# A hybrid attention block: the heads' stacked query and key operands by way of DRAM, and the causal mask inside the scan

## The chip, the cores and the metric

The kernel runs on one core of a Trainium2 chip. TensorE (PE) multiplies, VectorE (DVE), ScalarE (ACT) and GpSimd (POOL) do the elementwise work, SyncE (SP) issues most of the DMAs, and POOL issues some. The metric is the device time of one execution in microseconds (us); lower is better. A profile is one more execution, in which every instruction is recorded.

## The reference, cut to what matters

One layer of a decoder with 1024 tokens and a width of 1024. A norm and one wide projection give queries, keys and values for two kinds of attention, and two gates. The dilated attention has 12 heads in three groups; the stick-breaking attention has 8 heads. Both outputs are projected up, gated, added, projected again, and an MLP with a hidden width of 4096 follows.

```python
z = jnp.einsum('bhqd,bhkd->bhqk', q_blk, kt).astype(jnp.float32) * scale
causal = key_pos[None, :] < q_pos[:, None]
log_one_minus = jnp.where(causal, jax.nn.log_sigmoid(-z), 0.0)
suffix = lax.cumsum(log_one_minus, axis=3, reverse=True) - log_one_minus
log_a = jax.nn.log_sigmoid(z) + suffix
a = jnp.where(causal, jnp.exp(log_a), 0.0)
```

In the dilated heads the scores `q.k/8` get a bias that falls with the distance and go through a softmax over a window; groups 1 and 2 take every 4th or every 16th token, so their tokens are put into another order first.

## The kernel before, in words

Every float32 matmul is made of three products of halves: a value is rounded to a high part (an ACT copy, names with `h`), and the rest is the low part (a DVE subtraction, names with `l`).

**Two heads at a time.** A head is 64 wide and a tile has 128 partitions, so the projection of q (or k) for a pair of heads comes out as a [128, 1024] matrix with one head in partitions 0 to 63 and the other in 64 to 127. It comes in two column halves of 512 tokens. A score matmul of one head contracts over 128 partitions, and what lies in them is stacked: `qs` holds the high part of q on the head's own 64 partitions and the low part on the other 64, `kk` holds the high part of k on both, and `kl` holds the low part of k on the head's own 64 partitions and zeros on the others. `scores` (L850) then needs two matmuls, `qs` by `kk` and `qs` by `kl`.

**Who builds them.** In `qk_pair` (L800) the inner `sink` gets a column half of q or k. For every head it copies 64 partitions with ACT (k twice, once on each half), and subtracts 64 partitions with DVE. In groups 1 and 2 (pairs D2 to D5) each of these is two instructions, since the token order is changed by strided reads (`perm_dst`, L776). POOL clears the zero half of `kl` (L811). There are six dilated pairs, D0 to D5, and four stick-breaking pairs, S0 to S3. For the stick-breaking pairs the plain projection goes to DRAM first (`sb_pair`, `zdr`, L786 to 793), and `sb_load` (L795) reads it back when the heads are about to run; the `sink` works at that time.

**Stick breaking.** `sb_front` (L984) does, for each block of 128 queries: scores into PSUM, a sigmoid by ACT into `be`, on the block's last 128 columns a mask by POOL (`affine_select` writes 1 where the key is not before the query, L998), and a DVE scan from right to left (`tensor_tensor_scan`, multiply by `be` and add a zero, L1004). `sb_back` transposes the result, splits it and multiplies it by the values.

**What sets the order.** Nothing is issued as it is written. Class `Plan` (L65) records every operation, gives it a cost (`cost`, L186), a due time that follows from PE's order, and a window; `issue` (L222) then runs a list schedule in which each engine takes the ready operation that is due first, and emits a fixed order for each engine. A DMA is taken in the plan as 360 bytes per ns after 650 ns. All engines, SP's queue included, then run their own fixed order and wait on semaphores. `FILL` (L56) is the queue of projections that are slipped between the attention heads (`d1`, `s2` and so on); `ORDER` (L55) is the order of the heads. All working tiles share one pool of 102 slots.

Of the kernel before, what the change touches and what calls it, by code (L numbers as in the profile page):

```python
# [15 lines left out]
S = 1024  # L16
# [48 lines left out]
class Plan:  # L65
# [120 lines left out]
    def cost(eng, method, out, args, kw):  # L186
# [35 lines left out]
    def issue(self):  # L222
# [42 lines left out]
        ready = {}  # L265
# [116 lines left out]
def hybrid_block(ctx, tc, xT, w_t, w_vn, w_up, w_o, w_mi, w_mo, gains, bgate, out):  # L382
# [403 lines left out]
    zdr = dram.tile([4, 2, 2, 128, 512], F32, name="zdr")  # L786

    def sb_pair(n):
        def sink(i, c, src):
            if "PSUM" in str(src.tensor.space):  # L790
                src = keep(src)
            sync.dma_start(zdr[n, i, c], src)
        return seven((18 + n, 22 + n), sink)

    def sb_load(n, i, c):  # L795
        t = u2("sq", F32)
        sync.dma_start(t, zdr[n, i, c])
        return t

    def qk_pair(tq, tk, g, res, strassen, load=None):  # L800

        qs = [[u2("qs") for _ in range(2)] for _ in range(2)]
        kk = [[u2("kk") for _ in range(2)] for _ in range(2)]
        kl = [[u2("kl") for _ in range(2)] for _ in range(2)]
        res.extend((qs, kk, kl))

        for hd in range(2):
            for t in kl[hd]:  # L810
                pool.memset(f(t[64 * (1 - hd):64 * (1 - hd) + 64]), 0.0)  # L811

        def sink(i, c, ps):
            src = nat_src(ps, g)
            todo = []
            for hd in range(2):
                a, b = 64 * hd, 64 * (1 - hd)
                kld = perm_dst(kl[hd], g, c)
                for (dst, sl), (dl, _) in zip(perm_dst((kk if i else qs)[hd], g, c), kld):
                    sv = src[a:a + 64, sl] if g else src[a:a + 64]  # L820
                    if i:
                        act.activation(dst[a:a + 64], sv, AF.Copy)
                        act.activation(dst[b:b + 64], sv, AF.Copy)
                        todo.append((dl[a:a + 64], sv, f(dst[a:a + 64])))
                    else:
                        act.activation(dst[a:a + 64], sv, AF.Copy, scale=-0.125)
                        todo.append((dst[b:b + 64], sv, f(dst[a:a + 64])))
            for dst, sv, hi in todo:
                e = eng(SLE if load else DSE if "PSUM" not in str(ps.tensor.space) else "d")
# [5 lines left out]
        if load:  # L835
            for i in range(2):
                for c in range(2):
                    sink(i, c, load(i, c))
                    yield
            return  # L840
# [9 lines left out]
    def scores(ps, qk, hd, q0, k0, n):  # L850

        qs, kk, kl = qk
        qt, qo = qs[hd][q0 // 512], q0 % 512
        ki, ko = k0 // 512, k0 % 512
        pe.matmul(ps, qt[:, qo:qo + 128], kk[hd][ki][:, ko:ko + n], start=True, stop=False)
        pe.matmul(ps, qt[:, qo:qo + 128], kl[hd][ki][:, ko:ko + n], start=False, stop=True)
# [17 lines left out]
    def dil_head(g, slot, qk, vs, ut, dense):  # L874
# [5 lines left out]
        for c in range(2):  # L880
            es = {}
            for bk in range(2 if g < 2 else 1):
# [4 lines left out]
                if g < 2:  # L887
                    for j in range(2):
# [7 lines left out]
                        if k0 // 512 != (k0 + w - 1) // 512:  # L896
                            scores(sc[:, o0:o0 + 128], qk, hd, 128 * b, k0, 128)
# [652 lines left out]
```

## Time and profile before

| | us |
|---|---|
| median of 3 runs | 1509.33 |
| lowest and highest | 1506.43, 1511.13 |
| the profiled execution | 1508.43 |
| its span, first to last instruction | 1506.7 |

The page of the profile gives, for each engine, the time in which it was busy and the number of its instructions, then the granted TensorE clock, the DMA queues, the waits and the costliest groups of instructions. A view by stretches cuts the span and gives the same for each piece; a view of groups by form gives the mean time of one instruction of each shape. "DMA share" is the mean busy share of the core's 16 DMA engines, so that one engine alone is 0.06. Line 378 stands for all instructions, since the plan emits them there; so groups are told apart by the names of their tiles.

### The profile page before, as it was taken

How to read it: one execution, taken by the hardware profiler on the slowest of the kernel's cores; microseconds unless marked ns; L12 is line 12 of the kernel's file. 1: busy time of each engine (PE TensorE's matmuls, PEld its weight loads, DVE VectorE, ACT ScalarE, POOL GpSimd, SP SyncE). 2: the span in 40 equal slices, each digit the busy share in tenths (PEclk: the TensorE clock that was granted, in tenths of full speed). 3: DMA queues.
4: the chain of work that ended last, by engine and by line, in shares of the span. 5: the costliest groups of instructions: out<-in, count | busy, mean ns of one | idle time of the engine just before them, and what ended most of it. 6: DMA issues, size and time to landing. Idle time of an engine off the chain costs nothing.

```text
span 1506.7 us, 22489 instructions
## 1 busy us (share of the span) xinstructions
PE 1449.4 (96%) x7660; PEld 1231.9 (82%) x7660; DVE 1166.8 (77%) x2003; ACT 853.1 (57%) x1758; POOL 279.8 (19%) x322
## 2 busy tenths in 40 slices
PE   9999999899999999978999999999999999999997
PEld 8989887777787788756779978788888888888887
DVE  8798676987744498899999798666665969696876
ACT  8557667978544567764654464555555726262512
POOL 3674241222323333411140200000000000000000
PEclk9999999999999999999999999999999999999999
DMA  6403140131335644323513154444445917171603
GB/s 223 128 15 126 36 147 29 64 105 50 119 112 171 208 139 127 115 88 112 182 43 126 45 187 154 171 150 149 149 145 183 374 57 251 56 252 37 230 1 112
DMA packets 114900, 194.69 MB, mean 129 GB/s; under 512 B 14085, under 2 KB 29793, under 8 KB 114785
## 3 DMA queue, kind: packets, MB, share of 16 engines
q1 hardware_dynamic: 111456, 182.76, 36.0%
q0 software_dynamic: 3328, 10.49, 2.2%
q8 instruction: 60, 0.98, 0.3%
q14 instruction: 56, 0.45, 0.1%
HBM read 134.86 MB, written 58.34 MB: 128 GB/s over the span
## 4 chain that ended last, share of the span: by engine, by line
PE 68%; DVE 15%; ACT 7%; DMA 4%; issue 4%; POOL 1%; SPq 1%; DVEq 0%; POOLq 0%; ACTq 0%
PE bank L378 57%; PE vps L378 6%; DVE be L378 3%; ACT kk L378 3%; DVE ws L378 2%; DVE el L378 2%; PE po L378 2%; PE tr L378 1%; ACT e L378 1%; DMA vdr<-vt 1%; DVE tc L378 1%; DMA ws<-in_w_mi_dram 1%; PE sc L378 1%; DVE gl L378 1%; DVE hl L378 1%
## 5 line engine op out<-in xcount | busy, mean ns | idle before, releaser
L378 PE MATMUL bank<-hh,ws 128*128 128x512 f32 x1792 | 568.3, 394 | 5.3 <-ACT pk L378 2.7
L378 PEld LDWEIGHTS bank<-hh,ws 128*128 128x128 f32 x1792 | 336.4, 189 | 77.4 <-ACT pk L378 4.3
L378 DVE TENSOR_TENSOR ws<-ws 128x512 fp32r<-128x512 f32 (+3 forms) x520 | 344.8, 707 | 45.4 <-ACT ws L378 20.5
L378 PE MATMUL bank<-hl,ws 128*128 128x512 f32 x896 | 352.2, 393 | 0.0
L378 ACT ACTIVATE ws<-ws 128x512 fp32r<-128x512 f32 (+1 forms) x376 | 214.4, 607 | 161.9 <-PE bank L378 101.7
L378 PE MATMUL bank<-hi,ws 128*128 128x512 f32 (+1 forms) x976 | 285.1, 375 | 0.0
L378 PEld LDWEIGHTS bank<-hi,ws 128*128 128x128 f32 x976 | 179.3, 188 | 33.4
L378 PEld LDWEIGHTS bank<-hl,ws 128*128 128x128 f32 x896 | 169.2, 189 | 33.0 <-issue 0.2
L378 PE MATMUL bank<-lo,ws 128*128 128x512 f32 (+1 forms) x488 | 183.3, 376 | 0.0
L378 DVE TENSOR_TENSOR pk<-pk,bank 128x512 f32<-128x512 f32 x96 | 65.7, 685 | 106.9 <-ACT pk L378 53.2
L378 DVE TENSOR_TENSOR x<-x,bank 128x512 f32<-128x512 f32 (+1 forms) x180 | 106.5, 594 | 46.9 <-PE bank L378 46.2
L378 POOL TENSOR_TENSOR ws<-ws 128x512 f32<-128x512 f32 x64 | 91.2, 1432 | 189.0 <-DMA ws<-in_w_t_dram 76.9
L378 ACT ACTIVATE pk<-bank 128x512 f32<-128x512 f32 x100 | 59.2, 592 | 100.0 <-PE bank L378 98.8
L378 ACT ACTIVATE pk<-pk 128x512 f32<-128x512 f32 x96 | 60.4, 629 | 81.5 <-DVE pk L378 80.5
L378 PEld LDWEIGHTS bank<-lo,ws 128*128 128x128 f32 x488 | 91.9, 188 | 16.5
L378 DVE TENSOR_TENSOR_SCAN be<-be,zero 128x512 f32<-128x512 f32 (+3 forms) x96 | 89.3, 969 | 0.5 <-POOL be L378 0.2
L378 ACT ACTIVATE eh<-tr 128x512 fp32r<-128x512 f32 (+3 forms) x140 | 64.6, 498 | 22.0 <-PE tr L378 18.2
L378 PE MATMUL vps<-wv,hh 128*128 128x256 f32 x384 | 72.9, 286 | 0.0
L378 ACT ACTIVATE hi<-ub 128x512 fp32r<-128x512 f32 x98 | 59.3, 628 | 18.1 <-DMA ub<-udr 9.7
L378 PE MATMUL sc<-kk,qs 128*128 128x128 f32 (+2 forms) x196 | 60.5, 330 | 5.7 <-DVE el L378 4.2
L378 PE MATMUL bank<-msh,ws 128*128 128x256 f32 x352 | 65.0, 284 | 0.0
L378 PE MATMUL bank<-ooh,wu 128*128 128x512 f32 x192 | 64.3, 402 | 0.6 <-DVE ob L378 0.6
(164 smaller groups left out, 2411.8 us busy)
## 6 DMA issues: line engine op xcount, KB each, us to landing
ub<-udr SPq DMA_DIRECT2D x98, 256.0 KB
ws<-in_w_mi_dram SPq DMA_DIRECT2D x72, 256.0 KB
ws<-in_w_t_dram SPq DMA_DIRECT2D x64, 256.0 KB
udr<-tc SPq DMA_DIRECT2D x56, 256.0 KB
ws<-in_w_mo_dram SPq DMA_DIRECT2D x56, 256.0 KB
udr<-pk SPq DMA_DIRECT2D x48, 256.0 KB
gdr<-gt SPq DMA_DIRECT2D x32, 256.0 KB
gl<-gdr SPq DMA_DIRECT2D x32, 256.0 KB
```

The costliest lines, as they stand in the source:

```text
L378: o[1](*o[2], **o[3])
```

## The change

`qk_pair` no longer builds the stacked operands. Its `sink` makes the high part (`ph`) and the low part (`pl`) of all 128 partitions at once, one ACT and one DVE instruction (two each in groups 1 and 2), and stores both in a DRAM tensor, `pdr`, of 10 pairs. A new function, `head`, loads for each of the 20 heads the six tiles that `scores` needs. `qs` is loaded from the high and the low rows of the head, `kk` twice from the high rows of k, and `kl` twice from its low rows, so that the zeros and POOL's clearing are gone. The stick-breaking pairs go the same way, and `zdr`, `sb_pair` and `sb_load` are gone. In the scan of the block with the diagonal the added zero is replaced by a maximum with `tri`, a tile that is 1 where the mask is, and POOL's `affine_select` is gone. The plan's cost of a strided ACT copy changes too.

```diff
-            c = 0.833 * n * Plan.stride(out, args) + (51.0 if "PSUM" in str(args[1].tensor.space) else 93.0)
+            c = 0.833 * n * (2.4 if Plan.stride(out, args) > 1.5 else 1.0) + (51.0 if "PSUM" in str(args[1].tensor.space) else 93.0)
...
+    pdr = dram.tile([10, 2, 2, 2, 128, 512], F32, name="pdr")
+    def qk_pair(pair, tq, tk, g, strassen):
+        part = [[[None] * 2 for _ in range(2)] for _ in range(2)]
+        seen = [0, 0]
+        def store(i, t):
+            for j in range(2):
+                sync.dma_start(pdr[pair, i, j, t], f(part[i][j][t]))
...
-            for hd in range(2):
-                a, b = 64 * hd, 64 * (1 - hd)
-                kld = perm_dst(kl[hd], g, c)
-                for (dst, sl), (dl, _) in zip(perm_dst((kk if i else qs)[hd], g, c), kld):
-                    sv = src[a:a + 64, sl] if g else src[a:a + 64]
-                    if i:
-                        act.activation(dst[a:a + 64], sv, AF.Copy)
-                        act.activation(dst[b:b + 64], sv, AF.Copy)
-                        todo.append((dl[a:a + 64], sv, f(dst[a:a + 64])))
...
+            for (dst, sl), _ in zip(his, los):
                 if i:
-                    e.tensor_sub(dst, sv, hi)
+                    act.activation(dst, src[:, sl] if g else src, AF.Copy)
                 else:
-                    e.scalar_tensor_tensor(dst, sv, -0.125, hi, op0=ALU.mult, op1=ALU.subtract)
...
+            seen[i] += 1
+            if not g:
+                store(i, c)
+            elif seen[i] == 2:
+                for t in range(2):
+                    store(i, t)
...
+    def head(pair, hd):
+        rows = slice(64 * hd, 64 * hd + 64)
+        res = []
+        for name, i, js in (("qs", 0, (0, 1)), ("kk", 1, (0, 0)), ("kl", 1, (1, 1))):
+            ts = [u2(name) for _ in range(2)]
+            for t in range(2):
+                src = pdr[pair, i, :, t, rows] if js[1] > js[0] else \
+                    pdr[pair, i, js[0], t, rows].unsqueeze(0).broadcast_to([2, 64, 512])
+                sync.dma_start(f(ts[t]), src)
+            res.append(ts)
+        return res
...
-            o = (nk - 128) % 512
-            pool.affine_select(bes[-1][:, o:o + 128], bes[-1][:, o:o + 128], pattern=[[-1, 128]],
-                               compare_op=ALU.is_gt, fill=1.0, base=0, channel_multiplier=1)
...
+                if kc == nch - 1:
+                    dve.tensor_tensor_scan(bv, bv, tri[:, 512 - n:512][:, ::-1], initial=init, op0=ALU.mult, op1=ALU.max)
+                else:
+                    dve.tensor_tensor_scan(bv, bv, zero1.to_broadcast([128, n]), initial=init,
+                                           op0=ALU.mult, op1=ALU.add)
```

The source of a head's load is a list of 2 by 64 rows by 512 values, its destination a list of 128 rows; all loads of the kernel before have the same outermost count on both sides.

How the change moves instructions, at three places. First SP's queue where dilated pair D2 is prepared, before (`ws` are weight blocks, `gdr` and `udil` stores of gates and of heads' results):

```order
L378 DMA ws<-in_w_t_dram 128x512 x4
L378 DMA gdr<-gt 128x512 x3
L378 DMA ws<-in_w_t_dram 128x512 x4
L378 DMA udil<-ut 128x512 x2
L378 DMA ws<-in_w_t_dram 128x512 x4
L378 DMA gdr<-gt 128x512 x2
```

and after, from the same gate stores to the next weights:

```order
L378 DMA gdr<-gt 128x512 x3
L378 DMA pdr<-ph 128x512 x4
L378 DMA pdr<-pl 128x512 x2
L378 DMA kk<-pdr 128x1x512
L378 DMA pdr<-pl 128x512 x2
L378 DMA kk<-pdr 128x1x512 x3
L378 DMA qs<-pdr 128x1x512
L378 DMA kl<-pdr 128x1x512
L378 DMA qs<-pdr 128x1x512
L378 DMA kl<-pdr 128x1x512
L378 DMA qs<-pdr 128x1x512 x2
L378 DMA kl<-pdr 128x1x512 x2
```

Eight stores and the twelve loads of both heads now stand between the gate stores and the next four weight blocks, in one piece.

PE at the first scores of D2, before (`bank` is the accumulator of a projection):

```order
L378 MATMUL bank<-hh,ws 128x512 x2
L378 MATMUL bank<-hl,ws 128x512
L378 MATMUL bank<-hh,ws 128x512
L378 MATMUL sc<-kk,qs 128x128
L378 MATMUL sc<-kl,qs 128x128
L378 MATMUL sc<-kk,qs 128x256
L378 MATMUL sc<-kl,qs 128x256
```

and after:

```order
L378 MATMUL bank<-hl,ws 128x512
L378 MATMUL bank<-hh,ws 128x512 x2
L378 MATMUL sc<-kk,qs 128x128 x2
L378 MATMUL bank<-hl,ws 128x512
L378 MATMUL bank<-hh,ws 128x512
L378 MATMUL sc<-kl,qs 128x128
L378 MATMUL sc<-kk,qs 128x256
```

The scores stand at nearly the same place among the projections, and scores that wait for a load have the rest of PE's order behind them.

SP's queue where the first stick-breaking pairs are prepared, before (`sq` is a reloaded projection, `vraw` the values):

```order
L378 DMA n<-bdr 128x512
L378 DMA zdr<-pk 128x512
L378 DMA sq<-zdr 128x512 x2
L378 DMA zdr<-pk 128x512
L378 DMA sq<-zdr 128x512 x3
L378 DMA vraw<-vdr_82 127x128
```

and after:

```order
L378 DMA pdr<-pl 128x512
L378 DMA kk<-pdr 128x1x512
L378 DMA kl<-pdr 128x1x512
L378 DMA qs<-pdr 128x1x512
L378 DMA kk<-pdr 128x1x512
L378 DMA kl<-pdr 128x1x512
L378 DMA qs<-pdr 128x1x512
L378 DMA kk<-pdr 128x1x512
L378 DMA kl<-pdr 128x1x512
L378 DMA vraw<-vdr_82 127x128
```

Where a pair had four reloads, each of its two heads has six loads, and those of later heads follow one another.

## Rows read from the trace of the kernel before

**Rows 1.** The page's first part: busy time and share of each engine.

```profile
PE 1449.4 (96%) x7660; PEld 1231.9 (82%) x7660; DVE 1166.8 (77%) x2003; ACT 853.1 (57%) x1758; POOL 279.8 (19%) x322
```

**Rows 2.** By stretches: us from:to, length, busy us of each engine (instructions), clock, DMA.

```profile
core 0: us, PE busy (x) PEld busy (x) DVE busy (x) ACT busy (x) POOL busy (x), PEclk, DMA share, GB/s
100.00:400.00 300.00, 283.91 (x1560) 239.13 (x1559) 232.67 (x394) 224.64 (x529) 92.31 (x87) 0.99 0.23 77
400.00:520.00 120.00, 118.40 (x518) 96.54 (x517) 53.98 (x74) 54.43 (x95) 43.20 (x40) 1.00 0.48 157
520.00:720.00 200.00, 178.22 (x1006) 147.80 (x1006) 186.78 (x289) 134.20 (x290) 54.52 (x87) 0.96 0.40 122
860.00:1507.00 647.00, 635.05 (x2954) 530.50 (x2952) 482.52 (x856) 301.92 (x562) 4.77 (x6) 0.99 0.45 156
```

**Rows 3.** Groups by form: operation, shape, count | busy us, mean ns | idle before it.

```profile
L378 ACT ACTIVATE kk<-pk 64x256 fp32r<-64x256 f32 x64 | 40.0, 650 | 4.1 <-DVE pk L378 2.5 <-DVE ut L378 0.8
L378 ACT ACTIVATE kk<-sq 64x512 fp32r<-64x512 f32 x32 | 19.5, 624 | 2.3 <-DMA sq<-zdr 1.2 <-POOL wv L378 0.8
L378 DVE TENSOR_TENSOR kl<-pk,kk 64x256 fp32r<-64x256 f32 x32 | 18.6, 601 | 6.0 <-ACT kk L378 5.4
L378 DVE TENSOR_TENSOR kl<-sq,kk 64x512 fp32r<-64x512 f32 x16 | 13.5, 856 | 8.2 <-ACT kk L378 7.9
L378 DVE SCALAR_TENSOR_TENSOR qs<-sq,qs 64x512 fp32r<-64x512 f32 x16 | 10.7, 686 | 8.6 <-ACT qs L378 8.3
L378 DVE TENSOR_TENSOR_SCAN be<-be,zero 128x512 f32<-128x512 f32 x48 | 58.9, 1249 | 0.1
L378 POOL TENSOR_SCALAR_AFFINE_SELECT be<-be 128x128 f32<-128x128 f32 x64 | 37.4, 599 | 120.6 <-ACT be L378 116.4 <-DMA wb<-wdr 4.2
L378 POOL MEMSET kl<- 64x512 f32 x40 | 20.2, 521 | 32.0 <-DVE ws L378 14.0 <-PE po L378 9.0 <-PE sc L378 3.2
```

**Rows 4.** The DMA view: destination, source, queue, count, KB of each.

```profile
zdr<-pk SPq DMA_DIRECT2D x16, 256.0 KB
sq<-zdr SPq DMA_DIRECT2D x16, 256.0 KB
...
vraw<-vdr SPq DMA_DIRECT2D x4, 63.5 KB
```

**Rows 5.** SP's issues around 570 us: start us, us, queue, transfer, count.

```profile
564.45 1.50 SPq L378 DMA_DIRECT2D wb<-wdr  x2
569.79 0.24 SPq L378 DMA_DIRECT2D vraw<-vdr  x1
581.99 0.34 SPq L378 DMA_DIRECT2D wu<-in_w_up_dram  x1
```

**Rows 6.** By stretches of 1 us after the issue at 569.79, and 5 us.

```profile
571.00:572.00 1.00, 1.00 (x11) 1.00 (x10) 0.97 (x2) 1.00 (x2) 0.17 (x1) 1.00 0.06 19
572.00:573.00 1.00, 1.00 (x9) 0.86 (x8) 1.00 (x2) 0.98 (x3) 0.00 (x0) 1.00 0.07 22
573.00:574.00 1.00, 0.07 (x1) 0.00 (x0) 1.00 (x2) 0.99 (x3) 0.00 (x0) 1.00 0.10 30
574.00:575.00 1.00, 0.00 (x0) 0.00 (x0) 1.00 (x2) 0.55 (x1) 0.00 (x0) 1.00 0.00 0
575.00:580.00 5.00, 4.95 (x22) 4.36 (x23) 3.92 (x6) 3.60 (x7) 0.17 (x1) 0.66 0.00 2
```

**Rows 7.** By stretches, where 128-row transfers fill the DMA engines.

```profile
606.50:608.00 1.50, 1.50 (x9) 1.02 (x7) 0.82 (x2) 1.28 (x5) 0.00 (x0) 1.00 0.86 320
1150.00:1200.00 50.00, 50.00 (x223) 41.39 (x222) 41.36 (x68) 36.57 (x66) 0.00 (x0) 1.00 0.88 316
```

**Rows 8.** Tile qs, 225 to 262 us (pair D2): count, ns min/median/max, first and last start.

```profile
L378 PE MATMUL sc<-kl,qs x16: 222/279/335, 239.3 to 259.6; 128*128 128x128 f32 x8, 128*128 128x256 f32 x8
L378 ACT ACTIVATE qs<-bank x4: 366/372/379, 237.8 to 238.8; 64x256 fp32r<-64x256 f32 x4
```

**Rows 9.** Tile qs, 515 to 720 us (the stick-breaking heads), the same columns.

```profile
L378 PE MATMUL sc<-kk,qs x96: 220/392/774, 520.4 to 719.8; 128*128 128x512 f32 x48, 128*128 128x128 f32 x16, 128*128 128x256 f32 x16, 128*128 128x384 f32 x16
```

More of the change, by code (lines that the diff above doesn't have):

```diff
@@ L264, in issue @@
         live = set()
-        ready = {}
+        ready, heads = {}, {}
         for i in range(n):
@@ L784, in perm_dst @@
                 for i in range(2)]
[L786 to L807, printed above, removed]
-        for hd in range(2):
-            for t in kl[hd]:
-                pool.memset(f(t[64 * (1 - hd):64 * (1 - hd) + 64]), 0.0)
+    pdr = dram.tile([10, 2, 2, 2, 128, 512], F32, name="pdr")
@@ L813, in sink @@
+    def qk_pair(pair, tq, tk, g, strassen):
[4 more added lines that the diff above has]
+                sync.dma_start(pdr[pair, i, j, t], f(part[i][j][t]))
         def sink(i, c, ps):
+            for j in range(2):
+                for t in (range(2) if g else (c,)):
+                    part[i][j][t] = part[i][j][t] or u2("ph" if j == 0 else "pl")
             src = nat_src(ps, g)
-            todo = []
@@ L828, in sink @@
-            for dst, sv, hi in todo:
-                e = eng(SLE if load else DSE if "PSUM" not in str(ps.tensor.space) else "d")
+            e = eng(DSE if "PSUM" not in str(ps.tensor.space) else "d")
+            his, los = (perm_dst(part[i][j], g, c) for j in range(2))
+            for (dst, sl), _ in zip(his, los):
                 if i:
-                    e.tensor_sub(dst, sv, hi)
+                    act.activation(dst, src[:, sl] if g else src, AF.Copy)
                 else:
-                    e.scalar_tensor_tensor(dst, sv, -0.125, hi, op0=ALU.mult, op1=ALU.subtract)
@@ L835, in qk_pair @@
[L835 to L840, printed above, removed]
+                    act.activation(dst, src[:, sl] if g else src, AF.Copy, scale=-0.125)
+            for (dst, sl), (dl, _) in zip(his, los):
+                if i:
+                    e.tensor_sub(dl, src[:, sl] if g else src, f(dst))
+                else:
+                    e.scalar_tensor_tensor(dl, src[:, sl] if g else src, -0.125, f(dst), op0=ALU.mult, op1=ALU.subtract)
@@ L848, in qk_pair, with scores @@
                 yield
-    def scores(ps, qk, hd, q0, k0, n):
+    def head(pair, hd):
[9 more added lines that the diff above has]
+        return res
+    def scores(ps, qk, q0, k0, n):
         qs, kk, kl = qk
-        qt, qo = qs[hd][q0 // 512], q0 % 512
+        qt, qo = qs[q0 // 512], q0 % 512
         ki, ko = k0 // 512, k0 % 512
-        pe.matmul(ps, qt[:, qo:qo + 128], kk[hd][ki][:, ko:ko + n], start=True, stop=False)
-        pe.matmul(ps, qt[:, qo:qo + 128], kl[hd][ki][:, ko:ko + n], start=False, stop=True)
+        pe.matmul(ps, qt[:, qo:qo + 128], kk[ki][:, ko:ko + n], start=True, stop=False)
+        pe.matmul(ps, qt[:, qo:qo + 128], kl[ki][:, ko:ko + n], start=False, stop=True)
     def join(po, a, dst, view):
@@ L982, in hybrid_block, with sb_front @@
     ob = [[u2("ob", F32) for _ in range(4)] for _ in range(2)]
-    def sb_front(hd, c, qk, at):
+    tri = u2("tri", F32)
+    pool.memset(tri, 0.0)
+    pool.affine_select(tri[:, 384:512], tri[:, 384:512], pattern=[[-1, 128]], compare_op=ALU.is_gt, fill=1.0, base=0,
+                       channel_multiplier=1)
+    def sb_front(c, qk, at):
         def step(qi):
@@ L992, in step @@
                 sc = psc.tile([128, 512], F32, name="sc", tag="sc")
-                scores(sc[:, :n], qk, hd, 128 * qi, 512 * kc, n)
+                scores(sc[:, :n], qk, 128 * qi, 512 * kc, n)
                 be = u2("be", F32)
@@ L1116, in up @@
             yield
-    qk = {}
     queue = []
@@ L1163, in dense @@
                         fill_step()
-                dil_head(g, 2 * (n % 2) + hd, qk[f"D{n}"], vs, ut, dense)
+                dil_head(g, 2 * (n % 2) + hd, head(n, hd), vs, ut, dense)
             for c in range(2):
@@ L1168, in hybrid_block @@
             halves += [(n[0], i // 2, i % 2, int(x)) for i, x in enumerate(item.split(":")[1])]
-    ready = {}
+    ready, heads = {}, {}
     def front(i):
         pr, hd, c, _ = halves[i]
-        name = f"S{pr}"
         if pr not in ready:
             drain(f"V{3 + pr // 2}")
-            drain(name)
-            if name not in qk:
-                qk[name] = []
-                for _ in qk_pair(0, 0, 0, qk[name], False, lambda i, c: sb_load(pr, i, c)):
-                    pass
+            drain(f"S{pr}")
             ready[pr] = vs_load(3 + pr // 2, 128 * (pr % 2), 0, True)
+        if (pr, hd) not in heads:
+            heads[pr, hd] = head(6 + pr, hd)
         at[i] = []
-        return sb_front(hd, c, qk[name], at[i])
+        return sb_front(c, heads[pr, hd], at[i])
     def merge(*streams):
```

21 lines of the change are left out of this document (7 added, 14 removed).

## The prediction

> **What bounds the kernel now.** I read the engines' totals first: PE is busy for 1449.4 of 1506.7 us, so no more than 57 us can be won by any relief of the others [rows 1]. Then the stretches, to see where PE waits. From 860 us on it hardly does, and nothing of the change lies there [rows 2]. From 100 to 400 us, where the dilated heads run, PE is idle for 16.1 us of 300. From 520 to 720 us, with the stick-breaking heads, it is idle for 21.8 us of 200, and DVE is busy for 186.8 of them: DVE is the next bound in that stretch. So the attention stretches run close to PE's limit, and DVE's in the second; the DMA engines are lightly used in both, at shares of 0.23 and 0.40. The reader should keep two sums apart, what the change can give back (bounded by these idle times) and what its new transfers can take (bounded by nothing so far, since no head waits for a transfer now).
>
> **What the change removes.** By the groups by form, the copies into `kk` cost ACT 40.0 and 19.5 us in their two largest groups; one full-height copy takes the place of four of half height, so three quarters, 45 us, go. The subtractions into `kl` and `qs` halve: of 18.6, 13.5 and 10.7 us about 21 go from DVE. In the stick-breaking stretch all 24.2 us of the two groups that read `sq` go, since they are done when the pair is projected. POOL loses 37.4 us of masking and 20.2 us of clearing [rows 3]. POOL is idle most of the time, and the mask stood between the sigmoid and the scan, so its going shortens a chain that DVE's queue covers: worth nothing by itself while DVE is full. The scan with `tri` reads a second tile. At least it stays at 1249 ns for 512 columns, at most a plain two-operand pass comes on top, about 0.7 us each for the 64 that hold a diagonal. I take no change, since the scan already takes far longer per column than such a pass. The new cost of strided copies in the plan only moves instructions.
>
> **What it adds.** Per pair eight stores of 256 KB and twelve loads of 256 KB, which is 80 and 120 in all; 16 stores and 16 reloads by way of `zdr` and `sq` go [rows 4]. The stores have 128 rows on both sides, like most transfers here. From the stretches with full engines, 316 GB/s at a share of 0.88 and 320 GB/s at 0.86 are 22.4 and 23.3 GB/s for one busy engine [rows 7]; I use 23. Spread over 16 engines, 256 KB (262,144 bytes) take 0.71 us, over two 5.7 us, over one 11.4 us.
>
> How many engines does a head's load get? Its source counts 2, then 64 rows; its destination counts 128. No transfer in this trace has that shape, so this is the open cost, with ends 0.71 and 11.4 us. The nearest row is a load of 127 rows: it is issued at 569.79 us as SP's only transfer until 581.99 [rows 5], and in the next 4 us the DMA share is 0.06, 0.07, 0.10 and 0.00, at 19 to 30 GB/s [rows 6]. That is one engine of 16, for 63.5 KB [rows 4]. So a transfer of many rows isn't spread by its bytes; a count that 16 does not divide loses the engines. I read the same for a source that counts 2 on the outside, and take two engines, 5.7 us.
>
> The Trainium skill says so outright, on its page DMA: Bandwidth & Descriptors, section "Rules for kernel authors": a DMA whose outermost dimension counts c below 16, "e.g. a leading zero-stride broadcast of c copies", is confined to at most c engines. By that rule the load takes the two-engine price, and without it a reader who goes by the destination's 128 rows would sum at 0.71 us; the trace agrees with the rule for the 127 rows, and has nothing with unlike sides.
>
> **Where it lands, dilated pairs.** Twelve loads on two engines are 68 us. They can't start before the projection of the pair is done and stored (in groups 1 and 2 a store waits for both column halves), and SP's queue has all twelve in one piece right behind the stores, with the next weights behind them. In the trace D2's last part of q is written at 237.8 to 238.8 us and its last score starts at 259.6 [rows 8]; about 20 us of PE's work is what can cover the loads, and less where the new order draws the second head's scores forward. I take a cover of 17 us of 68. So about 51 us per pair are waited for, on PE, at scores that have all of PE's later work behind them. PE's order is fixed, so the next projection can't fill the hole, and its weights are behind the loads in SP's queue as well. Six pairs: 306 us. Some of the 16.1 us of old waits lie inside these; I take 300.
>
> **Stick-breaking pairs.** Eight heads of six loads are 48 by 5.7, 274 us, on the same two engines. The other traffic of the stretch adds to them, between 50 us and the 80 that the share of 0.40 over 200 us gives; I take 60, for the reloads through `zdr` are gone. These 334 us have to pass in a stretch that now takes 200 from the first score at 520.4 to the last at 719.8 [rows 9]. The stores of S1 to S3 are done early, but the loads follow one another in one queue, and the first head's are prepared only about 14 us ahead. So 120 us are added. Between, from 400 to 520 us, PE is idle for 1.6 us only, the loads have passed, and nothing changes.
>
> **The sum.** 1508.4 (the profiled execution, of which 1506.7 are span) plus 300 plus 120 is 1928 us; that execution is 0.9 us under the median. The relief of ACT, DVE and POOL falls into stretches that then wait for DMA, and I count none of it. After a wait the clock falls: behind a hole at 573 to 575 us it stood at 0.66 for 5 us, which is half of 2.4 GHz for part of it [rows 6]; some microseconds for each pair, of the size of the old waits that I did not take off in full. I say 1925.
>
> **The rivals.**
>
> Two engines, but hidden better. If the loads ran ahead so that the two engines never pause, only their total counts: 120 loads are 684 us, the other traffic of 100 to 720 us by its shares 69 + 58 + 80, or 207 us [rows 2], the 80 stores 57 us more, the old `zdr` traffic 23 us less. These 925 us against 620 add 305, 1813 us; with only some 120 us of the other traffic ahead of the last load, 1692. For it speaks that the pool has 102 slots and the stick-breaking loads stand early; against it that the dilated loads stand right behind their own projections. I put it at 1770.
>
> All 16 engines serve the loads (the other side, faster). Then a load is 0.71 us, and 44 MB more spread over 600 us are nothing to engines at shares of 0.23 and 0.40. DVE's 24.2 us leave the stretch that it bounds, and up to its 21.8 us of PE's idle time come back; I take 15 of these and 5 of the 16.1 us of the dilated stretch: 1488 us. The point that decides is the price of one load: at a cover of 17 us, twelve loads are free below 1.4 us each, and from there on every further 0.1 us costs about 7 us over six pairs. For it speaks that the destination has 128 rows; against it the 127-row load.
>
> The loads are spread, but the way through DRAM itself is late: a store must land before a load is issued and that one before the score. A few us for each dilated pair, against the same relief: 1504 to 1530, I put 1512.
>
> **How the numbers follow.** Chances: the forecast 0.64, its better hidden form 0.18, the faster case 0.13, the late round trip 0.05 (0.03 of it within the bound, 0.02 slower). The forecast's own range, from covers of 10 to 25 us a pair and loads of 5.4 to 6.2 us, is 1830 to 2040; with the better hidden form the range goes down to 1690, and 1690 to 2040 holds a little over 8 in 10. About 0.3% is what a measurement of this kernel can tell from no change. Faster by more than that 0.13, within it 0.03, slower 0.84.
>
> **What would show it.** Right: in the stretches of the attention heads PE's busy share falls to two thirds or less, its waits at `sc` (and at the weight loads before them) end with DMAs of `qs`, `kk` or `kl`; while these run alone the DMA share stands near 0.12, at some 45 GB/s; the last score comes near 1130 us instead of 720; the stretch after it keeps its length of about 787 us; ACT, DVE and POOL are busy for less. Wrong: a load that lands within 3 us of its issue, a DMA share well over 0.12 while only such loads run, or a last score at about 700 us. If the waits are there but in the dilated pairs only, the stick-breaking term is wrong; if a pair's wait is far from 51 us, the cover is.

## The result and the profile after

The changed kernel takes 2003.97 us (2001.61 to 2005.11), the kernel before, beside it, 1508.55 us. The ratio is 1.328, with a 95% interval of 1.326 to 1.331: 495 us slower. The forecast was 1925 in a range of 1690 to 2040.

The page of the changed kernel, its first part and the slices of the clock and of the DMA engines:

```profile
PE 1514.2 (76%) x7660; PEld 1281.9 (64%) x7660; DVE 1138.2 (57%) x1947; ACT 781.9 (39%) x1642; POOL 223.6 (11%) x220
...
PEclk9967769575957699867767799999999999999999
DMA  5313223132312244413242325224444358436232
```

Against [rows 1] PE has the same 7660 matmuls and went from 96% to 76% of the span. ACT lost 71 us of work, POOL 56 and DVE 29, and none of that shows in the time. PE itself is busy for 65 us longer with the same matmuls (1514.2 us against 1449.4): of the 497 us between the two profiled executions 432 are more idle time on PE, and 65 are work at a lower granted clock. The clock digits fall again and again in the first 23 slices of 50 us and are full behind them: the loss lies in the first 1200 us.

The view by stretches, cut where the kernel's parts end (columns as in [rows 2]):

```profile
100.00:689.00 589.00, 308.73 (x1455) 256.12 (x1454) 195.97 (x329) 161.20 (x411) 71.99 (x63) 0.71 0.25 87
689.00:845.00 156.00, 140.93 (x626) 116.01 (x625) 77.45 (x105) 70.78 (x134) 50.85 (x40) 0.95 0.44 149
845.00:1146.00 301.00, 134.10 (x684) 114.44 (x684) 104.31 (x163) 71.18 (x160) 14.22 (x16) 0.70 0.29 95
1146.00:1213.00 67.00, 59.78 (x319) 46.82 (x320) 63.59 (x101) 40.57 (x94) 0.00 (x0) 0.96 0.31 92
1213.00:2003.00 790.00, 773.09 (x3867) 655.77 (x3865) 613.10 (x1090) 375.02 (x702) 30.97 (x28) 0.99 0.42 145
```

The first row holds the dilated heads, whose last score starts at 689 us (387 before); PE is idle for 280 of 589 us. The second runs to the first stick-breaking score, 156 us (133 before). The third and fourth hold the stick-breaking heads, 368 us (200 in [rows 9]). The last is the rest, 790 us (787 before). The differences are 302, 23, 168 and 3 us, together 496; the first 100 us keep their length.

What PE waits for, in the view of waits over the whole span (us in all, times, longest):

```profile
PE sc L378 <- DMA qs<-pdr: 135.9, 13, 35.7
PE sc L378 <- DMA kl<-pdr: 85.4, 17, 13.2
PE tr L378 <- ACT be L378: 56.0, 2, 45.3
PE po L378 <- DVE el L378: 52.9, 8, 15.2
PE sc L378 <- DMA kk<-pdr: 39.7, 3, 23.9
```

Three of the five are scores that wait for a head's load, 261 us; all but 20 of them lie in the dilated stretch. The third, a single hole of 45.3 us, comes up below.

One dilated pair, D4, in SP's queue (start, duration, transfer, count), and what the chip does meanwhile:

```profile
541.68 9.91 SPq L378 DMA_DIRECT2D kk<-pdr  x3
551.64 5.00 SPq L378 DMA_DIRECT2D qs<-pdr  x1
556.73 4.95 SPq L378 DMA_DIRECT2D kl<-pdr  x1
561.78 4.96 SPq L378 DMA_DIRECT2D qs<-pdr  x1
566.78 5.00 SPq L378 DMA_DIRECT2D kl<-pdr  x1
571.87 10.00 SPq L378 DMA_DIRECT2D qs<-pdr  x2
581.92 10.68 SPq L378 DMA_DIRECT2D kl<-pdr  x2
592.94 6.52 SPq L378 DMA_DIRECT2D ws<-in_w_t_dram  x4
```

```profile
550.00:555.00 5.00, 0.00 (x0) 0.00 (x0) 0.00 (x0) 0.00 (x0) 0.00 (x0) 0.61 0.13 51
555.00:560.00 5.00, 0.00 (x0) 0.00 (x0) 0.00 (x0) 0.00 (x0) 0.00 (x0) 0.50 0.13 51
560.00:565.00 5.00, 0.00 (x0) 0.00 (x0) 0.00 (x0) 0.00 (x0) 0.00 (x0) 0.50 0.13 52
```

This is the mechanism in eleven lines. With two or three loads under way, SP can issue the next one only when one is done, every 5.0 us. Meanwhile no engine works at all, and the DMA share is 0.13, two engines of 16, at 51 GB/s: 262,144 bytes at that rate are 5.1 us. The next weights stand behind the twelve loads, as the order of SP's queue had it. The clock goes to 0.50, the 1.2 GHz level, as PE stands still.

That the loads queue behind each other, and don't go to different pairs of engines, shows in the share: it stays at 0.13 with several under way. The Trainium skill, page DMA: Bandwidth & Descriptors, section "Why a DMA increments its semaphore by 16 and not by 1", has both halves of this: the count is the largest number up to 16 that divides the outermost counts of both sides, and a DMA from SP takes the lowest-numbered engines of the core. The trace agrees with the count; the numbers of the engines do not show in it.

### The profile page after: what moved, and what is told of

The parts are those of the page before. It is cut to its first block, busy times and chain, and to the rows that moved or that the text cites. A ratio compares the mean times of both kernels' runs of the same rounds, so it can differ in the third digit from the quotient of the medians.

```text
span 2003.3 us, 22392 instructions
## 1 busy us (share of the span) xinstructions
PE 1514.2 (76%) x7660; PEld 1281.9 (64%) x7660; DVE 1138.2 (57%) x1947; ACT 781.9 (39%) x1642; POOL 223.6 (11%) x220
## 5 line engine op out<-in xcount | busy, mean ns | idle before, releaser
L378 PE MATMUL bank<-hh,ws 128*128 128x512 f32 x1792 | 578.2, 400 | 2.9 <-DVE pk L378 1.8
L378 PEld LDWEIGHTS bank<-hh,ws 128*128 128x128 f32 x1792 | 343.6, 193 | 76.5 <-DVE pk L378 3.5
L378 PE MATMUL sc<-kk,qs 128*128 128x128 f32 (+2 forms) x196 | 82.1, 429 | 209.9 <-DMA qs<-pdr 135.9
L378 PEld LDWEIGHTS sc<-kk,qs 128*128 128x128 f32 x196 | 50.7, 263 | 220.3 <-issue 193.5
L378 DVE SCALAR_TENSOR_TENSOR e<-steps,sc 128x384 f32<-128x384 f32 (+1 forms) x40 | 24.4, 618 | 258.2 <-PE sc L378 257.8
L378 PE MATMUL sc<-kl,qs 128*128 128x128 f32 (+2 forms) x196 | 75.3, 397 | 85.4 <-DMA kl<-pdr 85.4
L378 DVE TENSOR_TENSOR_SCAN be<-be,tri 128x128 f32<-128x128 f32 (+3 forms) x64 | 50.6, 810 | 112.8 <-ACT be L378 112.8
L378 PEld LDWEIGHTS sc<-kl,qs 128*128 128x128 f32 x196 | 51.2, 265 | 94.2 <-DMA kl<-pdr 92.2
L378 PE MATMUL tr<-ident,be 128*128 128x128 f32 x288 | 55.7, 304 | 68.2 <-ACT be L378 56.0
L378 ACT ACTIVATE e<-e,stat 128x128 f32<-128x128 f32 (+1 forms) x96 | 42.2, 443 | 166.6 <-DVE stat L378 166.6
```

The lines of the kernel that those rows point to most:

```text
L378: o[1](*o[2], **o[3])
```

## The experiments

The theory on trial: the loads' outermost count of 2 gives each of them two engines, and everything else follows. The rivals: the round trip through DRAM itself, the order of the plan, or the larger traffic.

**Each load cut in two.** The plan and its order stay; where a load stood, SP issues two of 64 rows, with 64 rows on either side.

```diff
+    def two(dst, src):
+        nc.sync.dma_start(dst[0:64], src[0])
+        nc.sync.dma_start(dst[64:128], src[1])
...
-                sync.dma_start(f(ts[t]), src)
+                plan.record("sync", "dma_start", two, (f(ts[t]), src), {})
```

> The changed kernel with every head load cut into two DMAs of 64 rows, one for each half of the destination; the bytes, the stores and the order of all engines are those of the changed kernel, and only the outer list of a load is another (64 rows on both sides instead of 2 by 64 against 128). Theory, two engines: the loads spread over 16 engines, land in about 3 us, the holes at the scores go, and with them all of the loss: 1475 to 1515 us, PE's busy share back at 95% or more. Rival, the volume or the way through DRAM: the same bytes go the same way, so about 2000 us stay. Rival, the new order of the plan: the order is kept, so about 2000 us stay as well.

Measured: 1535.55 us (1532.42 to 1539.39) against 1509.82, ratio 1.018 [1.016, 1.019]. The same bytes in twice as many DMAs took 468 us off the 2004. While these loads run the DMA share is 0.94 (284 to 296 us), so all 16 engines serve them. So the main cause lies in how a load is written, and not in its bytes, the way through DRAM or the plan's order. But this kernel was 20 us slower than the top of the expected range, and still 26 us slower than the kernel before: whether that is the price of the way through DRAM, the kernel with the rows outside tells below.

**Only the dilated pairs' loads cut.** The same edit for `pair < 6`; the stick-breaking loads stay on two engines.

> Only the loads of the six dilated pairs are cut in two; the eight stick-breaking heads keep theirs. Theory: the two parts of the loss are independent. The last dilated score comes at 390 us instead of 689, the stick-breaking part still takes what it took, about 190 us more than before from its first load to its last score: 1690 to 1720 us. Rival, the stick-breaking heads are late mainly because the dilated ones made the queue late: below 1600 us.

Measured: 1712.96 us, as expected. So the dilated loads cost 2004 - 1713 = 291 us, and the stick-breaking loads 1713 - 1536 = 177. These two differences add up by the way they are taken. That the parts are independent shows in the stretch: from the first to the last stick-breaking score it takes 366 us here (554.4 to 920.8 us), and 368 in the changed kernel.

**Four and eight engines.** One DMA for a load, with a source of 4 by 32 rows, then of 8 by 16.

```diff
+    def four(dst, src):
+        nc.sync.dma_start(dst, src[0, 0:32].unsqueeze(0).broadcast_to([4, 32, 512]))
...
+        nc.sync.dma_start(dst, src[0, 0:16].unsqueeze(0).broadcast_to([8, 16, 512]))
```

> Every head load stays one DMA of the same size, but its source counts 4 by 32 rows instead of 2 by 64 (the same 32 rows four times, so what the heads compute is not the reference's). Theory, the outer count sets the engines: four engines, 2.5 us a load instead of 5.0, 30 us a pair against a cover of 10 to 17; 80 to 120 us lost in the dilated pairs, 0 to 60 in the stick-breaking ones: 1570 to 1690 us. Rival, a repeated or stacked source is slow whatever its count: about 2000 us. Rival, any source whose list is unlike the destination's falls to one fixed slow path: about 2000 us.

> The changed kernel with each head load as one DMA whose source is read as 8 times 16 rows of one part (the operands then hold the wrong rows; bytes, count and place of the loads stay). Theory (the number of engines is the outermost count of the source): 8 engines, so 1.25 us of transfer for a load and 15 us for a pair, after 60 with two and 30 with four. Two gave 509 us over the 16-engine form and four 211, that is 51 and 21 us for each of ten pairs, so some 9 us of a pair's loads are covered, and 8 engines leave about 6 for each pair or, once they are under the cover, nothing: 1495 to 1560 us. Rival (few engines is all or nothing below 16): about 1700 us as with four, or more.

Measured: 1706.24 us with four, 1583.90 with eight, 16 and 24 us above their ranges. By stretches, while such loads run (first four, then eight):

```profile
303.00:308.00 5.00, 2.36 (x7) 1.67 (x8) 0.00 (x0) 0.00 (x0) 0.00 (x0) 0.50 0.26 102
```

```profile
268.00:270.00 2.00, 2.00 (x10) 1.67 (x9) 0.00 (x0) 0.00 (x0) 0.00 (x0) 1.00 0.53 204
```

DMA shares of 0.13, 0.26 and 0.53 are, to within a tenth, 2, 4 and 8 engines, and the rates 51, 102 and 204 GB/s follow: 25.5 GB/s for an engine each time. The number of engines is the outermost count of the source. That both runs ended above their ranges has to do with the clock as well as with the cover; the working is below.

**The 64 rows outside.** The most telling edit, two lines: the same loads, one DMA each, at the same place of the plan, but the source counts 64 rows on the outside and the two parts inside. The 128 rows of a tile then hold the parts by turns, in `qs` as in `kk` and `kl`, and a contraction doesn't care for the order.

```diff
-                src = pdr[pair, i, :, t, rows] if js[1] > js[0] else \
-                    pdr[pair, i, js[0], t, rows].unsqueeze(0).broadcast_to([2, 64, 512])
+                src = pdr[pair, i, :, t, rows].rearrange("j r n -> r j n") if js[1] > js[0] else \
+                    pdr[pair, i, js[0], t, rows].unsqueeze(1).broadcast_to([64, 2, 512])
```

> The changed kernel with one edit: the source of each head load is written with its 64 rows outermost and the two parts (high and low, or the one part twice) inside, so that the outermost count of the source is 64 and not 2. The bytes, the number of DMAs (one for each load) and their place in the plan stay; the rows of an operand now lie in another order in its tile, the same for query and key, so the product is the same sum. Theory (the engines of a load follow the outermost count of the source): the load runs on all 16 engines, lands 2 to 3 us after its issue as with the two cuts, and SP issues 12 instead of 24 DMAs for a pair, which takes some 7 us of SP's time out of each pair: 1505 to 1530 us, at or below the 1535.5 of the two cuts. Rival A (it is the destination's 128 rows against the 64 of the source, any difference of the two sides, that sends the load to few engines): 1700 to 2010 us. Rival B (one DMA with rows of 2 KB taken by turns from two places in DRAM is slow in itself): between, 1560 to 1700 us.

Measured: 1494.68 us (1493.91 to 1495.73) against 1511.14, ratio 0.990 [0.988, 0.991]. The kernel is 1.0% faster than the one before, 509 us faster than the changed one, and 10 us below the expected range. Its page, then SP's queue at pair D2, its stretches (100 to 400 us, and the stick-breaking heads) and PE's waits from 100 to 705 us:

```profile
PE 1446.2 (97%) x7660; PEld 1232.4 (83%) x7660; DVE 1135.4 (76%) x1947; ACT 779.4 (52%) x1642; POOL 228.2 (15%) x220
```

```profile
247.78 0.56 SPq L378 DMA_DIRECT2D qs<-pdr  x1
248.43 0.56 SPq L378 DMA_DIRECT2D kl<-pdr  x1
249.07 0.56 SPq L378 DMA_DIRECT2D qs<-pdr  x1
```

```profile
100.00:400.00 300.00, 288.89 (x1588) 244.87 (x1587) 217.10 (x359) 179.49 (x457) 86.11 (x74) 0.99 0.54 185
500.00:705.00 205.00, 188.74 (x1067) 157.67 (x1066) 172.22 (x271) 116.81 (x264) 23.88 (x22) 0.97 0.58 183
```

```profile
PE sc L378 <- DMA qs<-pdr: 2.6, 1, 2.6
PE sc L378 <- DMA kl<-pdr: 2.0, 3, 1.3
...
PE sc L378 <- DMA kk<-pdr: 0.4, 1, 0.4
```

SP issues a load in 0.56 us, the scores wait 5 us for loads in all where they waited 261, and from 100 to 400 us PE is busy for 288.9 us, against 283.9 in [rows 2]. So nothing is wrong with the way through DRAM, nor with the plan's order or the traffic. Against the loads cut in two, which move the same bytes on 16 engines too, it is 41 us faster. In that kernel's queue two issues stand for each of these:

```profile
291.12 0.44 SPq L832 DMA_DIRECT2D qs<-pdr  x1
291.62 0.59 SPq L833 DMA_DIRECT2D qs<-pdr  x1
```

That is 0.5 to 0.6 us of SP's queue more for each of 120 loads, with stores, weights and value loads behind them, and its scores wait 21 us for loads from 100 to 400 us alone (8.9, 6.0 and 5.9 for the three names). That the issues make the 41 us is argued from these rows; no run separates it. The Trainium skill, page DMA: Bandwidth & Descriptors, section "Rules for kernel authors", advises against two transfers to disjoint halves of the partitions and for one of 128, and the two runs bear it out. One transfer of 128 partitions is not enough by itself, though: the changed kernel's loads were that too, and they took 468 us more than the halves.

**The values from POOL's queue.** The 45.3 us hole from 863 to 908 us of the changed kernel looks like this in the view of waits from 689 to 1220 us, and in SP's queue:

```profile
POOL vraw L378 <- DMA vraw<-vdr: 138.1, 5, 82.8
...
ACT be L378 <- POOL vraw L378: 64.4, 4, 47.0
```

```profile
882.19 7.11 SPq L378 DMA_DIRECT2D kl<-pdr  x1
889.36 13.24 SPq L378 DMA_DIRECT2D vraw<-vdr  x2
```

ACT's next sigmoid waits for POOL, which waits 82.8 us for value rows, and these stand in SP's queue behind seven head loads. The edit issues them from POOL's queue.

```diff
+    def from_pool(dst, src):
+        nc.gpsimd.dma_start(dst, src)
...
-                    sync.dma_start(prev[1:128, 0], src[0:127])
+                    plan.record("sync", "dma_start", from_pool, (prev[1:128, 0], src[0:127]), {})
```

> The changed kernel, with its two-engine loads, and one edit: the loads of the values (vraw) of stick breaking are issued from POOL's queue and not from SP's, so that they no longer stand behind head loads. Theory (the stick-breaking term was too small by a hole of 45 us on PE at 863 to 908, where ACT waits for POOL's value work, which waits for a load that stood in SP's queue): the hole goes, less what then becomes the next wait, since 328 us of head loads still have to pass: 1945 to 1985 us against 2004. Rival (the loads alone set the length of the stretch, and the hole only lies where PE would have waited for a head load anyway): 1995 to 2010 us.

Measured: 1993.35 us, 8 us above the theory's range and 2 below the rival's, so nearer to the rival. The 10 us that were won lie between the first and the last stick-breaking score (357.8 us against 367.8). The wait moved one DMA on (the view of waits of this kernel, 680 to 1210 us):

```profile
PE po L378 <- ACT eh L378: 99.9, 8, 43.9
...
ACT eh L378 <- DMA sdr<-stt: 45.0, 1, 45.0
```

Now ACT waits 45.0 us for a small store that stands behind the same loads. The loads set the length of the stretch, as the run with only the dilated loads cut says (177 us), and whichever DMA stands behind them shows the hole. My theory of the hole fell but for these 10 us.

**Scans of the last pair, and of the first.** What is it, then, that makes the stretch 168 us longer and not 120? After the last head load lands, at 1146 us by its semaphore events, the last score is still 67 us away, and the row 1146:1213 above has DVE at 63.6 and PE at 59.8 of these 67 us. The forecast had nothing there. The same 67 us stand in the kernel with only the dilated loads cut (854 to 921) and in the one with the values from POOL (1135 to 1201). To see whether DVE sets it, scans of one pair were cut to 8 columns, with the plan's order kept.

```diff
+        def short(out, x, m, **k):
+            nc.vector.tensor_tensor_scan(out[:, :8], x[:, :8], m[:, :8], **k)
+        if pr == 3:
+            plan.record("dve", "tensor_tensor_scan", short, args, kw)
```

> The changed kernel, two-engine loads and order of the instructions as they are, but the scans of the last stick-breaking pair run over 8 columns instead of 128 to 512 (so the outputs of that pair are not those of the reference). The scans of all four pairs take 91 us of DVE, so this takes some 23 us off the last pair, less about 3 us that the short ones cost. Theory (after the last head load has landed, 67 us of work of the last heads are left, and DVE sets its length): 2004 - 20 = 1984 us, 1980 to 1992. Rival A (what comes after the last load is set by other loads or by PE, whose busy time there is 58.5 of 63 us): 1998 to 2006.

> The same with the first stick-breaking pair in place of the last. Theory (while the loads run they set the pace, and DVE's work there is covered): no change, 2000 to 2006 us. Rival B (DVE's total work counts wherever it stands, since the loads wait for buffers that DVE's work frees): the same 20 us as in the last pair, 1980 to 1992.

Measured: 1991.88 us for the last pair and 2001.74 for the first; the kernel before ran at 1504.09 beside them, 1.5 us below the lowest of its other runs. So the first pair's scans are covered by the loads, as expected. The last pair's run ends at the very edge of the expected range, and against the first pair's run, its neighbour, only half of the 20 us came. The stretch from the last landing to the last score, in that kernel and in the one with the first pair's scans cut:

```profile
1140.00:1204.00 64.00, 59.40 (x319) 48.35 (x320) 51.12 (x101) 40.80 (x94) 0.00 (x0) 0.93 0.32 96
```

```profile
1144.00:1211.00 67.00, 60.68 (x322) 48.22 (x323) 63.98 (x102) 41.05 (x94) 0.00 (x0) 0.94 0.29 92
```

DVE has 12.9 us less to do, and the stretch is 3 us shorter, for PE is busy for 59.4 of 64 us. Of the 9.9 us between the two runs 3.7 lie between the first and the last stick-breaking score and 3.2 behind; 3.0 lie ahead of the first of these scores, where the edit is not, so some microseconds of each are noise. What runs after the last load is the work of the last heads on both engines, and either alone would nearly fill it.

**The other parts alone.** What is the rest of the change worth? Three kernels answer that, and one goes on from the best. First the kernel before with only the mask as the scan's second operand:

> The kernel before with the second part of the change alone: the scan of the diagonal block takes the maximum with the tile that is 1 on the mask, and POOL's masking is gone. Theory: DVE is full in that stretch and hides POOL, so 0 to 6 us are won, 1502 to 1509 us, and a scan of 128x512 keeps its 1.16 us. Rival, POOL's step between the sigmoid and the scan is waited for by PE: 10 to 20 us are won. Rival, the scan pays for its second tile: its time rises by up to 0.7 us each, and the time by up to 30 us.

Measured: 1507.80 us, ratio 0.9985 [0.9974, 0.9995]. The scans with `tri` take 1230 ns for 512 columns, where those with the zero took 1249 in [rows 3] (the 1.16 us of the expectation is the median over scans of all widths):

```profile
L378 DVE TENSOR_TENSOR_SCAN be<-be,zero 128x512 f32<-128x512 f32 x32 | 40.5, 1293 | 0.0
L378 DVE TENSOR_TENSOR_SCAN be<-be,tri 128x512 f32<-128x512 f32 x16 | 19.7, 1230 | 0.6 <-ACT be L378 0.6
```

Then each half of the change, on the kernel before, with the rows outside; the plan's new cost of a strided copy goes with the dilated half:

> The kernel before with only the stick-breaking half of the change, its loads written with the 64 rows outermost: the dilated pairs keep their operands on chip as before. ACT and DVE make the high and low parts once for a pair, four DMAs of 256 KB store them, and a head loads six; the mask is in the scan. Theory (with all 16 engines the loads are hidden, and DVE, which is busy over 90% in that stretch, is relieved of the parts that were made per head): 1488 to 1508 us against 1509.8. Rival (the round trip through DRAM and the values' loads behind it in SP's queue delay the first scores as they do with the two cuts): 1512 to 1530 us.

> The kernel before with only the dilated half of the change, loads with the 64 rows outermost: the six dilated pairs go through DRAM, the stick-breaking pairs and their mask as before. Theory (the two halves add up: rows outside for all gave -16.4 us and the stick-breaking half with its mask -6.8): -9.6 us, 1498 to 1504 us. Rival (the relief of ACT and DVE in the dilated stretch is off the path there, and the gain of the whole comes of SP, ACT and DVE together): 1507 to 1512 us.

Measured: 1504.32 us, ratio 0.9961 [0.9946, 0.9977], for the stick-breaking half with its mask, and 1501.48, ratio 0.9949 [0.9935, 0.9963], for the dilated half. So 6.8 and 8.2 us; the whole gave 16.5. The halves add up to within 1.5 us.

Last the kernel with the rows outside and the values from POOL's queue, both edits as above:

> The changed kernel with the 64 rows outermost in the sources of the head loads, and the loads of the values of stick breaking from POOL's queue as well. Theory (with all 16 engines nothing of weight stands in SP's queue ahead of the values; POOL's longest wait for one is 17 us in that stretch, and PE waits on none of it): no change against the rows outside alone, 1490 to 1499 us. Rival (POOL's wait for the values is what DVE's 16% of idle time in that stretch comes from): 1478 to 1489 us.

Measured: 1487.19 us (1482.25 to 1495.67) against 1509.64, ratio 0.986 [0.983, 0.989]. This is the fastest kernel here, 1.4% below the kernel before, and 7.5 us below the rows outside alone, in the rival's range. Its runs are spread wider than the others, and the two intervals touch at 0.988. POOL's waits for value rows fell from 18.8 to 7.3 us in the stick-breaking stretch, but its profiled run is also 5 us ahead at the last dilated score (368.8 and 373.6 us), where the edit is not; between the first and the last stick-breaking score it wins 3 us (188.3 and 191.4). How much of the 7.5 us is the edit stays open.

## Why the prediction was right, and where its terms were off

**The engines.** Right, and it carries the whole result: two engines, a DMA share of 0.13 (forecast 0.12), 51 GB/s (45), waits at `sc` in the dilated stretch that end with DMAs of `qs`, `kk` and `kl`. The step from the 127-row load to the load of 2 by 64 was an inference to a shape that the trace didn't have; the runs with 4, 8 and 64 on the outside show it.

**The price of a load.** 5.7 us was too much; it is 5.0 to 5.1. The 23 GB/s for an engine came from stretches in which most of the 16 were busy [rows 7]. Two, four or eight engines alone move 25.5 each.

**The dilated term.** 300 us forecast, 302 measured, but by two errors that cancel: the loads were priced too high, and the clock was nearly left out. The stretch from 100 us to the last dilated score (read from the tile view of `qs`), with two, four and eight engines for a load, with the rows outside, and in the kernel before:

```profile
100.00:689.30 589.30, 309.03 (x1457) 256.42 (x1455) 195.97 (x329) 161.30 (x412) 71.99 (x63) 0.71 0.25 87
100.00:510.60 410.60, 301.56 (x1455) 252.36 (x1454) 194.71 (x328) 161.43 (x411) 71.92 (x63) 0.80 0.37 125
100.00:431.40 331.40, 290.95 (x1459) 245.56 (x1457) 195.44 (x328) 161.45 (x411) 74.26 (x65) 0.89 0.47 155
100.00:373.60 273.60, 262.49 (x1457) 222.82 (x1455) 193.71 (x328) 159.53 (x411) 72.53 (x64) 0.99 0.55 188
100.00:387.00 287.00, 270.91 (x1494) 228.47 (x1493) 221.70 (x381) 215.48 (x509) 86.05 (x83) 0.99 0.22 74
```

The fourth row is the measure, since its scores wait 5 us for loads in all. The table has the differences to it, divided by six pairs. A load's price is 262,144 bytes by the measured rate, and the cover is the time of twelve loads less PE's idle time.

| engines | one load, us | twelve | a pair is longer by | PE idle | PE busy longer | cover |
|---|---|---|---|---|---|---|
| 2 | 5.1 | 61 | 52.6 | 44.9 | 7.8 | 16 |
| 4 | 2.57 | 31 | 22.8 | 16.3 | 6.5 | 15 |
| 8 | 1.285 | 15 | 9.6 | 4.9 | 4.7 | 10 |

The cover of 17 us came out nearly as taken, at 16. PE waited for 45 us a pair and not 51, because twelve loads took 61 us and not 68. The other error has the other sign: the same matmuls kept PE busy for 309.0 us at a mean granted clock of 0.71, and for 262.5 at 0.99, which is 46.5 us or 7.8 for a pair. The prediction had "some microseconds for each pair" for this, and set them off against the old waits, of which it had left about 10 us in the sum. Six pairs at 52.6 us are 316. Of these 13 go off, since with the rows outside the stretch ends at 373.6 us and not at 387: 8 because 37 of PE's matmuls no longer stand in it (the next stretch has 42 more), and 5 because PE is idle for less. So 302. That the term met its number is luck. No run holds the clock up while the loads are slow: some of the 46.5 us would have turned into waiting, since scores that stand between two loads wait for the next one in any case, and how much is not shown.

With eight engines the cover is down to 10 us. I had taken it from the 20 us of PE's work between the last part of q and the last score of D2, but the same rows have that pair's first score at 239.3 us, 1.5 us behind the last part: the rest of the 20 us begins with scores, and these wait for loads themselves. So the point of decision in the rival of the 16 engines, 1.4 us for a load, was too high: at 1.285 us the kernel still lost 89 us to the 16-engine form.

**The stick-breaking term.** This is the term that was mis-sized: 120 us forecast, 168 measured. The loads took 328 us, from the issue at 818 to the landing at 1146 us (334 forecast). That these are so near is in part luck: at 5.1 us the 48 loads are 245 us (274 forecast), and 83 (60 forecast) are other transfers and pauses; from 909 to 944 us SP issues no head load at all. The lead was 27 us and not 14, since the first load is issued at 818.11 and the first score starts at 845.14. What failed is the end of the sum. It let the last score fall on the landing of the last load, and 67 us of PE's and DVE's work were still to come: 328 - 27 + 67 = 368, less 200. The rows showed the ground for it: DVE is busy for 187 of 200 us in that stretch [rows 2], 23 us for a head, and heads that waited together for their loads can't be worked off in no time. Two of SP's rows give the ends of the loads:

```profile
818.11 0.53 SPq L378 DMA_DIRECT2D kk<-pdr  x1
...
1131.61 0.52 SPq L378 DMA_DIRECT2D kl<-pdr  x1
```

The forecast had scores waiting for their loads here as well. Between the first and the last stick-breaking score PE is idle for 174 us, and only 4.6 of these are such a wait; most of the rest are waits for ACT and DVE (the view of waits from 845 to 1213 us). Behind them stand other DMAs: in the chain that ended last, 1056 to 1150 us, half of the time goes to loads of values and of gates, each 10 to 13 us from issue to landing, issued between the head loads in SP's queue.

```profile
PE tr L378 <- ACT be L378: 56.0, 2, 45.3
PE po L378 <- DVE el L378: 52.2, 6, 15.2
...
PE sc L378 <- DMA kl<-pdr: 4.6, 1, 4.6
```

```profile
1080.03 11.98 DMA vraw<-vdr
1137.15 10.48 DMA gl<-gdr
```

**Between.** Forecast as unchanged, measured 23 us longer; 14.9 of these are the first stick-breaking score's wait for its `qs`, which the forecast had taken as landed by then, and some 9 are PE's work that stood in the dilated stretch before (626 matmuls against 584, 140.9 us against 131.4). The stretch behind kept its length, as forecast. Of the 79 us between forecast and result 48 are the stick-breaking term, 23 this one, 5 the two small rests of the sum (2 and 3), and 3 its rounding from 1928 to 1925.

**The better hidden form.** It would have needed two engines that never pause. In the dilated stretch 72 loads of 5.1 us are 367 us; a share of 0.25 over 589 us leaves, beside these at 0.13, about 100 us of all 16 engines for stores and weights: so the two paused for some 120 us, an estimate. At D4 the first load is issued at 539.7 us, while the pair's last stores go out (538.0 to 541.6), as the forecast said: the loads did not run ahead.

**The relief.** Counted as nothing in the changed kernel, as work that lies under the waits; the terms above add up without it. The rival with 16 engines had priced it at 20 us, 1488 us in all; the kernel that makes this rival true takes 1494.7, with 8.2 us from the dilated half, where the rival had put 5, and 6.8 from the stick-breaking half, where it had put 15. The scan with the second operand costs no more, as taken.

**Two loose sums.** By the prediction's own terms the last score falls at 720 + 300 + 120 = 1140 us, not near 1130 (it came at 1213), and the low end of its own range, a cover of 25 us with loads of 5.4, near 1850 and not at 1830. Neither bears on the outcome.

## What to carry to other kernels

Before a DMA is moved or split, read the outermost count of both its sides: where the chip's DMA share stands at a sixteenth or an eighth while an engine waits, that count is the first suspect, and an order of the rows with a large count outside may cost nothing, since a contraction takes its rows in any order. A stretch that becomes bound by a queue ends not with the queue's last transfer but with the work that still hangs on it, so add the run-out of the next bound. When many DMAs share a slow queue, moving one waiting DMA out of it may only show the next. And a wait that brings the clock down costs more than its idle time: here 65 of 497 us were the same matmuls at a lower clock.

## What the runs showed of the hardware

- A few engines are each faster than all in company: with two, four or eight at work they moved 51, 102 and 204 GB/s, 25.5 for each by their number, and 24.1 to 24.5 by the busy share, which is the measure of the 22.4 and 23.3 with most of the 16 busy [rows 7]. In the kernel with the rows outside, where the loads fill all 16, it is 22.5 by that measure, 356 GB/s at a share of 0.99:

```profile
250.00:252.00 2.00, 2.00 (x11) 1.65 (x10) 0.00 (x0) 0.00 (x0) 0.00 (x0) 1.00 0.99 356
```

- SP does not run far ahead of slow transfers: behind two or three two-engine loads under way its next issue took 5.0 us, the time of one such load, in place of 0.5, and everything in its queue stood still with it.
- While PE did nothing in pair D4 (it stood idle from 548 to 570 us), its clock was granted at 0.61 from 550 to 555 us and at 0.50, the 1.2 GHz level, from there on, and the few scores between two loads ran at it: 415 ns in the median for a 128x128 score at 640 to 700 us, against 274 ns in the kernel with the rows outside.
